# Reordering the opening of a fused HGRN2 encoder layer

## The chip, the cores and the metric

One core of a Trainium2 chip runs the kernel. TensorE (PE) multiplies, VectorE (DVE), ScalarE (ACT) and GpSimd (POOL) do elementwise work, and SyncE (SP) issues the loads and stores. The time is device microseconds of one execution, the median of several runs.

## The reference

Two sequences (1024 and 256 tokens of 1024 channels, f32) pass through one layer with the same weights:

```python
shift, scale, gate = split(silu(c) @ ada_w + ada_b, 3)          # c: one row for each sequence
h = rms(x) * norm_g * (1 + scale) + shift
q, f_fw, f_bw, i, z = split(h @ hg_w_in, 5)                      # 1024 x 10240, 16 heads of 128
lb = cumsum(softmax(hg_lb, 0), 0)[0]
f = lb + (1 - lb) * sigmoid(f_raw); k = 1 - f; g = log(f)        # for each direction
o = gated_chunkwise(silu(q), k_fw, i, g_fw) + flip(gated_chunkwise(flipped ...))
y = (rms(o) * norm_g2 * silu(z)) @ hg_w_out
out = rms(x + gate * y) * final_g
```

## The kernel before

Products in f32 are made as three products of split operands: each of h and w is cast to a high part, and the low part is the difference (`hi*hi + hi*lo + lo*hi`). `split_w` (L113) splits a weight block: a ScalarE copy makes the high part, a POOL subtraction the low part. `make_h` (L184) modulates two of the eight 128-channel blocks of one segment of tokens and splits them: one block is modulated on ScalarE (L191), cast on VectorE (L193) and its low part made on POOL (L195); the other goes VectorE (L192), ScalarE (L194), VectorE (L196). The tokens form three segments of 512, 512 and 256 (si = 0, 1, 2).

The opening (L228 to L325) is written under a manual schedule: each engine takes its instructions in the order of the text, SP its loads too. It does this:

- Small rows are loaded (`crow`: the conditioning; `lbrow`: the forget-gate bounds; `abn`: bias and norm gain), then x in blocks j of 128 tokens (`load_x`, tile `xj`, 4 buffers) and raw weight blocks (`fetch_raw`, tile `raw`, 2 buffers).
- `norm_x(j)` (L161): ScalarE squares a block and takes the root of its mean (L167, L168), VectorE takes the reciprocal and scales the block in place (L169, L170).
- `transpose_x(j)` (L172): eight TensorE transpositions in two halves, each into a PSUM bank; VectorE copies the first half to `xT`, ScalarE the second (L181).
- `load_mod(r)`, `mod_mm(r)`, `mod_tr(r)`: shift and scale of channel blocks 2r and 2r+1 (r = 0 to 3). Four loads of 512 KB (tile `aw`, 7 buffers), 64 small TensorE products, a VectorE copy, a TensorE transposition and two small VectorE instructions that write `mod`.
- `first_project(r, accs)` (L219): for each pair (i, si), six products (two channel blocks, three part products) of weight block i (0 is `wq`, 1 is `wff`) with segment si. All r add up in six banks `p_acc` (`pf` in the trace).

In the order before, `row(j)` normalises block j+2, transposes block j and loads block j+4; all eight blocks of the long sequence go first, with the loads of `aw0`, `wff` and part of `aw1` among them. Then come `mod_mm(0)`, `make_h` for r = 0, the first products, blocks 8 and 9, and three rounds, each with `mod_mm(r)`, `make_h` of the three segments and 36 products. The third weight block, `wv`, is split in two parts, the first in round 3, the second (into the weight buffer of `wq`, there being three) in the middle of the last products. The softmax of the forget-gate bounds (L309 to L325) ends the opening.

After it the main part begins with the product `pv` (L443). There TensorE's order is again that of the text, and a planner orders the other engines. PSUM has eight banks: three with tag pj, two tu, two sc, one ob. A tile waits for a buffer of its tag to come free.

Of the kernel before, what the change touches and what calls it, by code (L numbers as in the profile page):

```python
# [9 lines left out]
F32 = mybir.dt.float32  # L10
# [7 lines left out]
DRAM = bass.MemoryType.DRAM  # L18

P = 128  # L20
# [17 lines left out]
LEAD = 5  # L38
# first and last 128-token blocks of the two sequences
FIRST = (0, 8)  # L40
# [4 lines left out]
def kernel(  # L45
# [38 lines left out]

# [1 line left out]
    ident = const.tile([P, P], F32, name="ident")  # L86
# [32 lines left out]

    # weight blocks in the order in which the tensor engine takes them  # L120
    order = []
# [22 lines left out]

# [1 line left out]
    p0 = tc.alloc_tile_pool(name="p0", bufs=1)  # L146
# [4 lines left out]
    def load_x(j):  # L151
        xts[j] = p0.tile([P, D], F32, tag="xj", bufs=4, name=f"xj{j}")
        sp.dma_start(xts[j], xs[j])

    def load_mod(r, pieces=range(4)):
        # shift and scale of two of the eight channel blocks
        for k0, i in [(0, 0), (0, 1), (4, 0), (4, 1)][pieces[0]:pieces[-1] + 1]:
            aws[r, k0, i] = p0.tile([P, 4, 256], F32, tag="aw", bufs=7, name=f"aw{r}_{k0}_{i}")
            sp.dma_start(aws[r, k0, i], ada3[:, k0:k0 + 4, i * D + r * 256:i * D + (r + 1) * 256])

    def norm_x(j):  # L161
        """128 rows of x over their rms."""
        xj = xts[j]
        sq = p0.tile([P, D], F32, tag="sq", bufs=1, name=f"sq{j}")
        ssum = p0.tile([P, 1], F32, tag="ssum", bufs=4, name=f"ssum{j}")
        rst = p0.tile([P, 1], F32, tag="rst", bufs=4, name=f"rst{j}")
        act.activation(sq, xj, AF.Square, accum_out=ssum)  # L167
        act.activation(rst, ssum, AF.Sqrt, bias=eps_t, scale=1.0 / D)  # L168
        dve.reciprocal(rst, rst)  # L169
        dve.tensor_scalar_mul(xj, xj, rst)  # L170

    def transpose_x(j):  # L172
        xj = xts[j]
        si = min(j // 4, 2)
        c = slice(j * P - SEGS[si][0], (j + 1) * P - SEGS[si][0])
        for h in range(2):
            xp = ps.tile([P, 512], F32, tag=("tu", "sc")[h], bufs=2, name=f"xp{j}_{h}")
            for i in range(4):
                k = 4 * h + i
                pe.transpose(xp[:, i * P:(i + 1) * P], xj[:, k * P:(k + 1) * P], ident)  # L180
            (act.copy if h else dve.tensor_copy)(  # L181
                xT[si][:, 4 * h:4 * h + 4, c], xp.rearrange("p (i c) -> p i c", i=4))

    def make_h(si, r):  # L184
        """Channel blocks 2 r and 2 r + 1 of the modulated rows, split in two parts."""
        grp = 0 if SEGS[si][0] < TP else 1
# [11 lines left out]
    def mod_mm(r):  # L198
        # two channel blocks of shift and scale in four column tiles
        acc = mod_ps[:, (r % 2) * 256:(r % 2) * 256 + P]  # L200
# [8 lines left out]
    def mod_tr(r):  # L209
        tr = mod_ps[:, (r % 2) * 256 + P:(r % 2 + 1) * 256]  # L210
        pe.transpose(tr, mrows[r], ident)
        # mod[:, s, i, r]: shift of channel block i, then norm_g * (1 + scale), for prompt and sample
        i2 = slice(2 * r, 2 * r + 2)
# [5 lines left out]
    def first_project(r, accs):  # L219
        """Part of the projections by the first two weight blocks."""  # L220
        for i, si in accs:
# [6 lines left out]
    with tc.manual_schedule():  # L228
        crow = p0.tile([2 * KT, P], F32, name="crow")
        sp.dma_start(crow[:KT], c_prompt.rearrange("o (k p) -> (o k) p", p=P))  # L230
        sp.dma_start(crow[KT:], c_sample.rearrange("o (k p) -> (o k) p", p=P))
        lbrow = p0.tile([2 * NH + 1, P], F32, name="lbrow")
        sp.dma_start(lbrow[:2 * NH], hg_lb.rearrange("l (h p) -> (l h) p", p=P))
        sp.dma_start(lbrow[2 * NH:], hg_norm_g)
        abn = p0.tile([24, P], F32, name="abn")
        sp.dma_start(abn[:16], ada_b[0, :2 * D].rearrange("(a p) -> a p", p=P))
        sp.dma_start(abn[16:], norm_g.rearrange("o (a p) -> (o a) p", p=P))
        for j in range(4):
            load_x(j)
        raws[0] = fetch_raw(0)  # L240

        lb_ps = tu_bank("lb_ps")
        pe.transpose(lb_ps[:, 96:112], crow, ident[:16, :16])
        act.activation(csT, lb_ps[:, 96:112].rearrange("p (c k) -> p k c", c=2), AF.Silu)
        pe.transpose(lb_ps[:, :2 * NH + 1], lbrow, ident[:2 * NH + 1, :2 * NH + 1])
        pe.transpose(lb_ps[:, 64:88], abn, ident[:24, :24])
        dve.tensor_copy(lbT, lb_ps[:, :2 * NH + 1])
        abT = p0.tile([P, 3, KT, 1], F32, name="abT")
# [3 lines left out]

        def row(j):
            if j + 2 < 8:
                norm_x(j + 2)
            transpose_x(j)
            if j + 4 < NT:
                load_x(j + 4)

        norm_x(0)  # L260
        norm_x(1)
        for j in range(8):
            row(j)
            if j == 2:
                split(0, raws[0])
            if j == 3:
                load_mod(0)
                raws[1] = fetch_raw(1)
            if j == 5:
                load_mod(1, (0, 1, 2))  # L270
            if j == 6:
                split(1, raws[1])
        mod_mm(0)
        load_mod(1, (3,))
        mod_tr(0)
        make_h(0, 0)
        make_h(1, 0)
        for i in range(2):
            p_acc[i, 0] = pj_bank(f"pf{i}_0")
        norm_x(8)  # L280
        norm_x(9)
        first_project(0, ((0, 0), (1, 0)))
        row(8)
        row(9)
        for i in range(2):
            p_acc[i, 1] = ps.tile([P, 512], F32, tag="sc", bufs=2, name=f"pf{i}_1")
        make_h(2, 0)
        for i in range(2):
            p_acc[i, 2] = tu_bank(f"pf{i}_2")[:, :256]
        for r in range(1, 4):  # L290
            mod_mm(r)
            if r < 3:
                load_mod(r + 1)
            first_project(r - 1, ((0, 1),))
            mod_tr(r)
            if r == 3:
                raws[2] = fetch_raw(2)
                wv = [split_w(*raws[2][0])]
            for si in range(3):
                make_h(si, r)  # L300
            first_project(r - 1, ((1, 1), (0, 2), (1, 2)))
            if r < 3:
                first_project(r, ((0, 0), (1, 0)))
        first_project(3, ((0, 0), (0, 1), (0, 2), (1, 0)))
        ready[2] = wv + [split_w(*raws[2][1])]
        first_project(3, ((1, 1), (1, 2)))

        # forget-gate lower bound: softmax over the two rows of hg_lb
        e0 = p0.tile([P, NH], F32, name="e0")  # L309
# [9 lines left out]
        dve.tensor_tensor(e0, e0, e1, ALU.mult)  # L319
        # sigmoid(x) = (1 + tanh(x / 2)) / 2; the factor 2 of silu is kept in q and taken out of k  # L320
        dve.tensor_scalar(f_scale, e0, -0.5, 0.5, ALU.mult, ALU.add)
# [5 lines left out]
    def gate_rows():  # L327
        """The gate of the residual branch, kept in DRAM until the last phase."""
        aws, acc = {}, []
# [30 lines left out]

# [1 line left out]
    pp = tc.alloc_tile_pool(name="pp", bufs=1, reuse_waits="tile")  # L362
# [91 lines left out]
    def gates(e, d):  # L454
        """Decays of one direction and the key factors."""
        for si in seg_order["ff" if d == 0 else "fb"]:
# [4 lines left out]
        for si in seg_order["ff" if d == 0 else "fb"]:  # L461
# [21 lines left out]
            dec_t[e, d, si] = ds_  # L483
            # of two neighbouring chunks, the later queries in scan order meet the earlier keys
            # directly, and both meet the state at the start of the pair
            dve.tensor_tensor(x4[:, :, ca], u4[:, :, ca], k4[:, :, ca], ALU.mult)
# [18 lines left out]
    def attention(e):  # L505
        """Pieces of one head's attention, in the order in which the tensor engine takes them."""
        kts, sc_bank = {}, {}
# [65 lines left out]
        def out(b):  # L573
# [3 lines left out]
            if si not in obs:  # L577
                if si == 2:
                    # the free half of the bank of the scores
                    obs[si] = sc_bank[0][:, 2:].rearrange("p n c -> p (n c)")  # L580
                else:
                    obs[si] = ps.tile([P, 512], F32, tag="ob", bufs=1, name=f"ob{e}_{si}")
                left[si] = sl // P
# [49 lines left out]

# [1 line left out]
    HALF = NH // 2  # L635
# [47 lines left out]
    with tc.manual_schedule(engines={PE}):  # L683
# [5 lines left out]
        gates(0, 0)  # L689
        # two banks of scores: what no product writes is masked and only has to hold something  # L690
        sc_banks = [ps.tile([P, 4, P], F32, tag="sc", bufs=2, name=f"sc{i}") for i in range(2)]
# [138 lines left out]
```

## Time and profile before

| | us |
|---|---|
| median of 3 runs | 1742.09 (1742.04 to 1742.49) |
| span of the profiled execution | 1741.6 |
| PE busy | 1692.4 (97%) |
| DVE busy | 1014.0 (58%) |
| ACT busy | 775.8 (45%) |
| POOL busy | 578.6 (33%) |

The profiled execution's own time is not listed apart from its span, from the first to the last instruction; the median of the runs lies 0.5 us above it. Busy shares are averages over a span in which the opening and the main part differ. Rows of the timeline give the start in us, the duration, the engine, the line, and in brackets the idle time before with what ended it. Matmuls overlap, so the distance of two starts is the cost of one in a row of them.

### The profile page before, as it was taken

The numbers are of one execution on the slowest core, as the hardware profiler recorded it, in microseconds if no ns is written. First come the engines' busy times: TensorE is split into PE (matmuls) and PEld (weight loads), VectorE is DVE, ScalarE is ACT, GpSimd is POOL, SyncE is SP. The second block draws the span as 40 slices with busy tenths as digits, with TensorE's granted clock in tenths as the row PEclk, the third lists the DMA queues.
The fourth block names the chain that finished last, engine by engine and source line by source line (L and its number), as shares of the span: only waits on it lengthen the run. The fifth ranks groups of instructions, "written<-read, shape, count | busy, mean of one in ns | idle before, by whom it ended". The sixth has DMA issues, their size and how long they took to land.

```text
span 1741.6 us, 28354 instructions
## 1 busy us (share of the span) xinstructions
PE 1692.4 (97%) x11511; PEld 1461.6 (84%) x11511; DVE 1014.0 (58%) x2223; ACT 775.8 (45%) x1197; POOL 578.6 (33%) x547
## 2 busy tenths in 40 slices
PE   5999999999999999999999999999999999899998
PEld 4797789888988898889888998889888988788886
DVE  5646664667566754764477447744775466834322
ACT  5443534463545454545454435533463446542210
POOL 1532433352334233433344334333333333610000
PEclk8999999999999999999999999999999999999999
DMA  8311311011011011111111111111111100564310
GB/s 279 121 38 62 98 34 43 28 41 36 25 52 37 28 37 40 37 40 37 40 31 46 31 43 34 34 37 38 36 40 34 43 17 13 169 209 153 123 51 27
DMA packets 121268, 103.06 MB, mean 59 GB/s; under 512 B 3929, under 2 KB 108466, under 8 KB 121138
## 3 DMA queue, kind: packets, MB, share of 16 engines
q1 hardware_dynamic: 121138, 101.26, 18.3%
q8 instruction: 90, 1.47, 0.3%
q14 instruction: 40, 0.33, 0.1%
HBM read 85.50 MB, written 15.74 MB: 58 GB/s over the span
## 4 chain that ended last, share of the span: by engine, by line
PE 70%; DVE 19%; ACT 3%; issue 3%; DMA 0%; POOL 0%; DVEq 0%; ACTq 0%; POOLq 0%
PE pv L443 13%; PE pfb L421 12%; PE y L674 12%; PE pff L421 12%; PE pq L421 7%; PE pz L421 3%; PE ob L592 3%; DVE g L466 3%; DVE ku L473 2%; DVE qe L472 2%; PE sc L550 2%; DVE ke L489 2%; PE up L531 1%; DVE s L538 1%; PE kt L519 1%
## 5 line engine op out<-in xcount | busy, mean ns | idle before, releaser
L443 PE MATMUL pv<-wv_h,h_hi 128*128 128x256 f32 x640 | 181.2, 283 | 0.0
L443 PE MATMUL pv<-wv_l,h_hi 128*128 128x256 f32 x640 | 181.1, 283 | 0.0
L443 PE MATMUL pv<-wv_h,h_lo 128*128 128x256 f32 x640 | 181.1, 283 | 0.0
L522 DVE COPY kts<-kt 128x512 f32<-128x512 f32 (+2 forms) x96 | 48.3, 503 | 204.3 <-PE kt L519 204.3
L487 POOL TENSOR_TENSOR ku<-xx,dec 128x256 f32<-128x256 f32 (+1 forms) x96 | 74.7, 779 | 230.1 <-DVE dec L480 151.6
L466 DVE TENSOR_TENSOR_SCAN g<-reset,g 128x512 f32<-128x512 uint8 (+1 forms) x96 | 100.8, 1075 | 83.8 <-ACT g L458 83.8
L421 PE MATMUL pz<-h_hi,wz_h 128*128 128x512 f32 (+1 forms) x384 | 148.5, 387 | 0.0
L421 PE MATMUL pff<-h_hi,wff_h 128*128 128x512 f32 (+1 forms) x360 | 141.6, 393 | 0.0
L421 PE MATMUL pq<-h_hi,wq_h 128*128 128x512 f32 (+1 forms) x360 | 141.1, 392 | 0.0
L421 PE MATMUL pz<-h_hi,wz_l 128*128 128x512 f32 (+1 forms) x384 | 136.7, 356 | 0.0
L421 PE MATMUL pz<-h_lo,wz_h 128*128 128x512 f32 (+1 forms) x384 | 136.5, 356 | 0.0
L421 PE MATMUL pfb<-h_hi,wfb_h 128*128 128x512 f32 (+1 forms) x384 | 136.2, 355 | 0.0
L421 PE MATMUL pfb<-h_lo,wfb_h 128*128 128x512 f32 (+1 forms) x384 | 136.0, 354 | 0.0
L421 PE MATMUL pfb<-h_hi,wfb_l 128*128 128x512 f32 (+1 forms) x384 | 135.8, 354 | 0.0
L421 PE MATMUL pq<-h_hi,wq_l 128*128 128x512 f32 (+1 forms) x360 | 128.6, 357 | 0.0
L421 PE MATMUL pff<-h_hi,wff_l 128*128 128x512 f32 (+1 forms) x360 | 128.6, 357 | 0.0
L421 PE MATMUL pq<-h_lo,wq_h 128*128 128x512 f32 (+1 forms) x360 | 128.2, 356 | 0.0
L421 PE MATMUL pff<-h_lo,wff_h 128*128 128x512 f32 (+1 forms) x360 | 128.1, 356 | 0.0
L615 POOL TENSOR_TENSOR z<-z,rs 128x512 f32<-128x512 f32 (+1 forms) x48 | 54.1, 1127 | 212.2 <-ACT rs L614 211.0
L443 PEld LDWEIGHTS pv<-wv_l,h_hi 128*128 128x128 f32 x640 | 122.9, 192 | 0.0
L443 PEld LDWEIGHTS pv<-wv_h,h_lo 128*128 128x128 f32 x640 | 122.9, 192 | 0.0
L443 PEld LDWEIGHTS pv<-wv_h,h_hi 128*128 128x128 f32 x640 | 122.9, 192 | 0.0
(196 smaller groups left out, 4598.9 us busy)
## 6 DMA issues: line engine op xcount, KB each, us to landing
xj<-in_x_prompt_dram SPq DMA_DIRECT2D x16, 512.0 KB, 4.5
wq_r<-in_hg_w_in_dram SPq DMA_DIRECT2D x16, 512.0 KB, 3.8
aw<-in_ada_w_dram SPq DMA_DIRECT2D x16, 512.0 KB, 10.2
wff_r<-in_hg_w_in_dram SPq DMA_DIRECT2D x16, 512.0 KB
wv_r<-in_hg_w_in_dram SPq DMA_DIRECT2D x16, 512.0 KB, 3.5
wfb_r<-in_hg_w_in_dram SPq DMA_DIRECT2D x16, 512.0 KB
wz_r<-in_hg_w_in_dram SPq DMA_DIRECT2D x16, 512.0 KB
wo_r<-in_hg_w_out_dram SPq DMA_DIRECT2D x16, 512.0 KB, 4.7
```

Source lines behind the costliest of these rows:

```text
L421: pe.matmul(acc[:, :sl], a[:, k, :], h[si][:, k, :], start=n == 0, stop=n == 3 * KT - 1)
L443: pe.matmul(acc[:, :2 * P], h[si][:, k, c], a[:, k % 4, :], start=n == 0, stop=n == 3 * KT - 1)
L466: dve.tensor_tensor_scan(gs, reset[:, :sl], gs, 0.0, ALU.mult, ALU.add)
L472: dve.tensor_tensor(chunks(qe), g3, g3[:, :, mid:mid + 1].broadcast_to([P, nch, C]), ALU.subtract)
L473: dve.tensor_tensor(chunks(ku), g3[:, :, last:last + 1].broadcast_to([P, nch, C]), g3, ALU.subtract)
L487: pool.tensor_tensor(u4[:, :, ca], x4[:, :, ca], dec[:, :, cb].broadcast_to([P, nb, C]), ALU.mult)
L489: (pool if e == NH - 1 and d == 1 else dve).tensor_tensor(ke, ke, k, ALU.mult)
L522: dve.tensor_copy(kt[:, c], tp[:, c])
L550: pe.matmul(sps[c * C:(c + 1) * C, i, c * C:(c + 1) * C], ke[:, o:o + C], qe[:, o:o + C], start=True, stop=True)
L592: pe.matmul(ob[:, c], l, r, start=n == 0, stop=n == len(ops) - 1)
L615: pool.tensor_tensor(u, u, rs, ALU.mult)
L674: pe.matmul(y_bank(j, n), u[:, e % HALF, :], w[e][:, n * 512:(n + 1) * 512], start=first and e == 0, stop=last and e == NH - 1)
```

## The change

The loads of `abn` and of the first modulation weights (`load_mod(0)`) are issued ahead of x, six blocks of x can be loaded at once instead of four and eight pieces `aw` instead of seven, and `lbrow` is loaded later. The reserve in on-chip memory for descriptors written by software falls to 1024 bytes a partition. `mod_mm(0)` is issued ahead of the first block of x; the transpositions use the banks tu and pj instead of tu and sc, since the banks sc now belong to `p_acc[i, 1]` from the beginning. The loop of rows gives way to a list in which normalisation, transposition, modulation, `make_h` and first products alternate. In addition, comments and docstrings are removed.

```diff
-        xts[j] = p0.tile([P, D], F32, tag="xj", bufs=4, name=f"xj{j}")
+        xts[j] = p0.tile([P, D], F32, tag="xj", bufs=6, name=f"xj{j}")
...
-            aws[r, k0, i] = p0.tile([P, 4, 256], F32, tag="aw", bufs=7, name=f"aw{r}_{k0}_{i}")
+            aws[r, k0, i] = p0.tile([P, 4, 256], F32, tag="aw", bufs=8, name=f"aw{r}_{k0}_{i}")
...
-            xp = ps.tile([P, 512], F32, tag=("tu", "sc")[h], bufs=2, name=f"xp{j}_{h}")
+            xp = tu_bank(f"xp{j}_{h}") if (2 * j + h) % 3 else pj_bank(f"xp{j}_{h}")
...
+        load_mod(0)
+        for j in range(4):
+            load_x(j)
+        raws[0] = fetch_raw(0)
+        for j in range(4, 6):
+            load_x(j)
+        load_mod(1)
         lbrow = p0.tile([2 * NH + 1, P], F32, name="lbrow")
...
-        def row(j):
-            if j + 2 < 8:
-                norm_x(j + 2)
-            transpose_x(j)
-            if j + 4 < NT:
-                load_x(j + 4)
-
+        mod_mm(0)
         norm_x(0)
         norm_x(1)
-        for j in range(8):
-            row(j)
-            if j == 2:
-                split(0, raws[0])
-            if j == 3:
-                load_mod(0)
-                raws[1] = fetch_raw(1)
-            if j == 5:
-                load_mod(1, (0, 1, 2))
-            if j == 6:
-                split(1, raws[1])
-        mod_mm(0)
-        load_mod(1, (3,))
+        transpose_x(0)
+        load_x(6)
         mod_tr(0)
+        norm_x(2)
+        transpose_x(1)
+        load_x(7)
+        norm_x(3)
+        transpose_x(2)
+        raws[1] = fetch_raw(1)
+        load_x(8)
+        split(0, raws[0])
+        norm_x(4)
+        transpose_x(3)
+        load_x(9)
+        load_mod(2)
         make_h(0, 0)
+        norm_x(5)
+        transpose_x(4)
+        first_project(0, ((0, 0),))
+        transpose_x(5)
+        mod_mm(1)
+        load_mod(3)
+        norm_x(6)
+        mod_tr(1)
+        transpose_x(6)
+        norm_x(7)
+        make_h(0, 1)
+        transpose_x(7)
+        split(1, raws[1])
         make_h(1, 0)
-        for i in range(2):
-            p_acc[i, 0] = pj_bank(f"pf{i}_0")
+        first_project(1, ((0, 0),))
+        first_project(0, ((1, 0), (0, 1)))
         norm_x(8)
         norm_x(9)
-        first_project(0, ((0, 0), (1, 0)))
-        row(8)
-        row(9)
-        for i in range(2):
-            p_acc[i, 1] = ps.tile([P, 512], F32, tag="sc", bufs=2, name=f"pf{i}_1")
+        make_h(1, 1)
+        first_project(1, ((1, 0),))
+        transpose_x(8)
+        transpose_x(9)
+        first_project(0, ((1, 1),))
         make_h(2, 0)
+        raws[2] = fetch_raw(2)
+        pe.transpose(lb_ps2 := mod_ps[:, 128:128 + 2 * NH + 1], lbrow, ident[:2 * NH + 1, :2 * NH + 1])
+        dve.tensor_copy(lbT, lb_ps2)
+        mod_mm(2)
+        first_project(1, ((0, 1),))
+        mod_tr(2)
...
-        for r in range(1, 4):
-            mod_mm(r)
-            if r < 3:
-                load_mod(r + 1)
-            first_project(r - 1, ((0, 1),))
-            mod_tr(r)
-            if r == 3:
-                raws[2] = fetch_raw(2)
-                wv = [split_w(*raws[2][0])]
-            for si in range(3):
-                make_h(si, r)
-            first_project(r - 1, ((1, 1), (0, 2), (1, 2)))
-            if r < 3:
-                first_project(r, ((0, 0), (1, 0)))
-        first_project(3, ((0, 0), (0, 1), (0, 2), (1, 0)))
+        make_h(0, 2)
+        make_h(2, 1)
+        first_project(1, ((1, 1),))
+        make_h(1, 2)
+        first_project(0, ((0, 2), (1, 2)))
+        wv = [split_w(*raws[2][0])]
+        first_project(2, ((0, 0), (1, 0)))
+        mod_mm(3)
+        make_h(2, 2)
+        first_project(1, ((0, 2), (1, 2)))
+        mod_tr(3)
+        first_project(2, ((0, 1),))
+        for si in range(3):
+            make_h(si, 3)
+        first_project(2, ((1, 1), (0, 2), (1, 2)))
+        first_project(3, ((0, 0), (1, 0)))
         ready[2] = wv + [split_w(*raws[2][1])]
-        first_project(3, ((1, 1), (1, 2)))
+        first_project(3, ((0, 1), (1, 1), (0, 2), (1, 2)))
...
-    nc = _bacc.Bacc("TRN2", target_bir_lowering=False, num_devices=1)
+    nc = _bacc.Bacc("TRN2", target_bir_lowering=False, num_devices=1, dynamic_dma_scratch_size=1024)
```

## Rows read from the trace of the kernel before

**Rows 1.** Busy time by stretch: opening and rest (us; engines, granted clock, DMA share, GB/s).
```profile
0.00:80.00 80.00, 57.88 (x493) 46.73 (x494) 47.12 (x88) 41.92 (x75) 26.22 (x25) 0.89 0.63 205
80.00:1741.60 1661.60, 1634.53 (x11021) 1414.82 (x11019) 966.92 (x2136) 733.87 (x1123) 552.35 (x524) 1.00 0.17 52
```
**Rows 2.** Busy time by stretch: two of 5 us in the opening.
```profile
20.00:25.00 5.00, 3.54 (x17) 2.96 (x16) 3.90 (x8) 4.35 (x10) 1.27 (x1) 0.50 1.01 352
...
35.00:40.00 5.00, 4.07 (x9) 2.89 (x10) 4.50 (x6) 3.12 (x7) 2.78 (x2) 0.50 1.10 349
```
**Rows 3.** Waits, 0 to 90 us: who waited for whom, us, times, longest.
```profile
PE xp L180 <- DVE xj L170: 6.0, 1, 6.0
...
ACT sq L167 <- DMA xj<-in_x_prompt_dram: 5.0, 4, 3.3
ACT wff_h L116 <- DMA wff_r<-in_hg_w_in_dram: 4.4, 1, 4.4
```
**Rows 4.** Timeline: the first block of x, from its load to its copy.
```profile
2.97 1.78 SPq L153 DMA_DIRECT2D xj<-in_x_prompt_dram  x4
...
6.51 1.06 ACT L167 ACTIVATE sq<-xj 128x1024 f32<-128x1024 f32 x1 [3.33 <-DMA xj<-in_x_prompt_dram]
...
7.74 1.28 ACT L168 ACT_TABLE_LOAD   x1
...
10.37 5.26 PE L180 MATMUL xp<-ident,xj 128*128 128x128 f32 x24 [5.97 <-DVE xj L170]
...
12.37 0.59 ACT L181 COPY xT<-xp 128x512 f32<-128x512 f32 x1 [0.31 <-PE xp L180]
```
**Rows 5.** Timeline of PE: two later groups of eight transpositions.
```profile
15.98 1.10 PE L180 MATMUL xp<-ident,xj 128*128 128x128 f32 x8 [0.35 <-DVE xT L181]
...
19.06 1.97 PE L180 MATMUL xp<-ident,xj 128*128 128x128 f32 x8 [1.98 <-DVE xT L181]
```
**Rows 6.** Timeline: a weight split on POOL beside a scaling on DVE.
```profile
18.92 2.36 POOL L117 TENSOR_TENSOR wq_l<-wq_r,wq_h 128x1024 fp32r<-128x1024 f32 x1 [17.55 <-ACT wq_h L116]
...
20.44 1.38 DVE L170 TENSOR_SCALAR xj<-xj,rst 128x1024 f32<-128x1024 f32 x1
```
**Rows 7.** Timeline: low part of make_h(1,0) on POOL; first products at two pitches.
```profile
37.19 1.29 POOL L195 TENSOR_TENSOR h_lo<-xT,h_hi 128x512 fp32r<-128x512 f32 x1 [0.70 <-DVE h_hi L193]
...
37.56 0.63 PE L225 MATMUL pf<-h_hi,wq_h 128*128 128x512 f32 x1
...
37.99 0.63 PE L225 MATMUL pf<-h_lo,wq_h 128*128 128x512 f32 x1
...
53.16 0.39 PE L225 MATMUL pf<-h_hi,wff_h 128*128 128x512 f32 x1
53.39 0.40 PE L225 MATMUL pf<-h_lo,wff_h 128*128 128x512 f32 x1
```
**Rows 8.** Timeline: third modulation product, its addition, a low part behind it, first pv.
```profile
53.95 1.93 PE L203 MATMUL mod_ps<-aw,csT 128*2 128x128 f32 x64
...
57.62 0.17 DVE L215 TENSOR_TENSOR mod<-mod_ps,abT 128x8 f32<-128x8 f32 x1 [1.38 <-PE mod_ps L211]
...
64.39 0.74 POOL L195 TENSOR_TENSOR h_lo<-xT,h_hi 128x256 fp32r<-128x256 f32 x1 [1.16 <-DVE h_hi L193]
...
79.39 0.28 PE L443 MATMUL pv<-wv_h,h_hi 128*128 128x256 f32 x1
```
**Rows 9.** Timeline: second part of wv, softmax, q's evacuation.
```profile
76.05 1.05 ACT L116 CAST wv_h<-wv_r 128x1024 fp32r<-128x1024 f32 x1 [1.46 <-PE pf L225]
...
77.18 2.40 POOL L117 TENSOR_TENSOR wv_l<-wv_r,wv_h 128x1024 fp32r<-128x1024 f32 x1 [2.01 <-ACT wv_h L116]
...
78.77 0.84 DVE L317 TENSOR_TENSOR e<-e,e 128x16 f32<-128x16 f32 x1 [2.93 <-ACT e L316]
...
81.09 0.69 DVE L405 SCALAR_TENSOR_TENSOR q<-q,pf 128x512 f32<-128x512 f32 x1
```
**Rows 10.** Waits of PE, 80 us to the end: the largest.
```profile
PE kt L519 <- DVE s L538: 6.9, 16, 1.0
```

More of the change, by code (lines that the diff above doesn't have):

```diff
@@ L231 @@
         sp.dma_start(crow[KT:], c_sample.rearrange("o (k p) -> (o k) p", p=P))
+        abn = p0.tile([24, P], F32, name="abn")
+        sp.dma_start(abn[:16], ada_b[0, :2 * D].rearrange("(a p) -> a p", p=P))
+        sp.dma_start(abn[16:], norm_g.rearrange("o (a p) -> (o a) p", p=P))
+        load_mod(0)
[5 more added lines that the diff above has]
+        load_mod(1)
         lbrow = p0.tile([2 * NH + 1, P], F32, name="lbrow")
@@ L234 @@
         sp.dma_start(lbrow[2 * NH:], hg_norm_g)
[L235 to L240, printed above, removed]
         lb_ps = tu_bank("lb_ps")
@@ L244 @@
         act.activation(csT, lb_ps[:, 96:112].rearrange("p (c k) -> p k c", c=2), AF.Silu)
-        pe.transpose(lb_ps[:, :2 * NH + 1], lbrow, ident[:2 * NH + 1, :2 * NH + 1])
         pe.transpose(lb_ps[:, 64:88], abn, ident[:24, :24])
-        dve.tensor_copy(lbT, lb_ps[:, :2 * NH + 1])
         abT = p0.tile([P, 3, KT, 1], F32, name="abT")
@@ L251 @@
         dve.memset(mod_ps, 0.0)
-        def row(j):
-            if j + 2 < 8:
-                norm_x(j + 2)
-            transpose_x(j)
-            if j + 4 < NT:
-                load_x(j + 4)
+        for i in range(2):
+            p_acc[i, 0] = pj_bank(f"pf{i}_0")
+            p_acc[i, 1] = ps.tile([P, 512], F32, tag="sc", bufs=2, name=f"pf{i}_1")
+        mod_mm(0)
         norm_x(0)
         norm_x(1)
-        for j in range(8):
-            row(j)
-            if j == 2:
-                split(0, raws[0])
-            if j == 3:
-                load_mod(0)
-                raws[1] = fetch_raw(1)
-            if j == 5:
-                load_mod(1, (0, 1, 2))
-            if j == 6:
-                split(1, raws[1])
```

## The prediction

> **What bounds the kernel now.** I read the busy time by stretch first. After 80 us TensorE is busy 1634.5 of 1661.6 us; before that, 57.9 of 80 [rows 1]. The order after 80 us is not edited, so the question is when the first product of the third weight block (`pv`) can start: 79.39 us now [rows 8]. Next the waits of the opening: ScalarE waits 5.0 us for rows of x and 4.4 us for the raw `wff`, and TensorE 6.0 us before its first transposition [rows 3]. The stretches show loads at 349 to 352 GB/s with the engines' share at or over 1 [rows 2], so 512 KB take 1.5 us. Thus the first half of the opening waits for loads. The change attacks these; what counts is which wait ends last in their place.
>
> **Loads.** The 16 `aw` pieces, ten x blocks and four raw weight loads are the same 15.7 MB. Four `aw` loads now precede x: 4 x 1.5 = 6.0 us, less 0.7 us for the two `lbrow` issues moved behind. x0 landed at 6.51, when its Square started [rows 4]; it will land near 11.8. `aw0` lands near 10.2, and the first modulation product (1.93 us at full clock [rows 8]) ends before x0 is normalised. At 1.5 us a load x4 lands at 19, `aw1` at 27, x7 at 30, `wff` at 31, `aw3` at 46 to 48. SP's later issues wait for transpositions of rows 0 to 3 and for the second modulation product, which come before their place in that stream or at most some 2 us after it. So no wait for loads remains behind x0. The reduced descriptor reserve only makes room for the buffers; every load is issued on SP's queue. I cost it at nothing: the queue's waits, not POOL, would show if that were wrong.
>
> **Chain to the first half of h.** Every engine takes its list in order, so I follow it.
> - x0 to first transposition took 3.86 us including one table load of 1.28 [rows 4]; so transposition at 15.7, and 2.5 us per later row from Square to transposition. Eight transpositions take 1.10 us at full clock and 1.97 at half [rows 5]; a ScalarE copy 0.59, Square 1.06 [rows 4].
> - Before, rows were normalised two ahead. Now ScalarE holds the order copy 0, norm 2, copy 1, norm 3, copy 2, cast of wq, norm 4. The copy of row 0 starts at 17.6, Square 2 at 18.1, its transposition at 20.6; copy 2 at 21.7 to 22.5 (by the clock), the cast of wq, Square 4 at 23.2 to 24.0.
> - `wq_l` then runs on POOL, 2.36 us. The row scale that began under such a piece took 1.38 us and ended 0.54 us after it [rows 6]; so scale 4 ends at 26.2, and copy 3 (VectorE) behind it at 26.8. make_h(0,0) needs this copy; its low part ends near 30.1.
> - The first product group holds TensorE behind that low part: six products at 0.43 us pitch (half clock [rows 7]), to 32.4. Transposition 5 is queued behind it (34.1), copy 5 and with it Square 6 behind that (34.9). Before, these rows met no product.
> - mod_mm(1) is next, 34.1 to 36.8 (1.9 at full clock, nearly twice that at half by the ratio in [rows 5]; I take 2.7). Its copy stands ahead of scale 6 on VectorE: scale 6 at 38.1, transposition 6 at 39.0, Square 7 at 39.8, scale 7 at 42.2.
> - make_h(0,1) ends on VectorE at 45.0, copy 7 at 45.5. The cast of wff lets `wff_l` occupy POOL from 45.0 to 47.3, so both VectorE pieces of make_h(1,0) end at 47.6 and 48.0. Its low part (1.29 us [rows 7]) ends at **49.3**.
>
> The same piece ended at 37.19 + 1.29 = 38.5 before [rows 7]: 10.8 us later. In exchange TensorE has by then done the second modulation product and two groups that came later before. Transpositions now share three PSUM banks instead of four; each half waits for the copy three halves earlier, which at this pace has ended, so up to row 7 this costs nothing.
>
> **From there to the product pv.** TensorE's work left at 49.3 is the rest of one group (1.2) and 28.6 us: 12 wide groups of six products at 0.23 (16.6; the pitch at full clock [rows 7]), 8 narrow ones at half that (5.7), two modulation products (3.8), 16 transpositions at 0.11 (1.8) and 0.7 of small ones. Dense, it would end at 79.1. But VectorE and POOL also have rows 8 and 9 to scale, make_h(1,1) and make_h(2,0). Row 9's second half waits for a TU bank: 0.5 us if it takes the bank that ScalarE frees, 2.1 if the one that VectorE frees; I take 0.5, since a bank freed earlier is nearer to what the row order of the copies gives. The scale for channel blocks 4 and 5 is added at 59.4 against 57.62 [rows 8]. From that instruction to pv it took 79.39 - 57.62 = 21.8 us. The new order has one half-size make_h more there (1.6 us: 0.74 on POOL [rows 8] and three pieces on VectorE), and the third modulation addition no longer waits for TensorE (1.4 us); I take 21.7, and 20 to 23.5 as ends. pv can start at **81.1**, 1.7 later.
>
> **The end of the opening.** `wv` part 1 takes wq's weight buffer. Before, all wq products were issued ahead of four last wff groups, and the cast at 76.05 left `wv_l` ready at 79.58 [rows 9]. pv needs it 13 products of 0.12 after its start, 80.95: 1.4 us to spare. Now wq's (0,2) is next to last: it ends 0.7 before pv may start, and `wv_l` takes another 3.5 us from cast to end. It arrives at 81.1 - 0.6 + 3.5 = 84.0, needed at 82.7: a new stall of **1.4 us**. The softmax follows that cast on ScalarE, so q's evacuation (VectorE row at 81.09 [rows 9]) falls 2.6 us further behind and pv's second bank comes 0.1 to 0.8 late: **0.4**. These two edits are ordered wait for wait; the bounds are 0 and 2.4.
>
> **Sum.** +1.7 + 1.4 + 0.4 = +3.5 us on a profiled span of 1741.6, hence 1745.1. The median of the runs, 1742.09, lies 0.5 above the span; so 1745.6. `lbT`'s move (two small instructions, under mod_mm) and the comments cost nothing. The planner that orders the other engines after the opening may settle differently: TensorE's largest wait there is 6.9 us in 16 pieces [rows 10]; I take 0, with 2 either way.
>
> The clock has a rule against it. Rows of TensorE: eight transpositions at 15.98 ran at full clock after a dense run of 24, those at 19.06 at half after an idle stretch [rows 5]. The Trainium skill, "TensorE: Matmul & The Clock Gate", Part 4: PE-mode transpose, says that the full clock does not engage for transposes. This trace disagrees: the dense run brought it on. By that rule all eight rows would run at half clock, pv would be some 0.7 us later and the sum 1746.3.
>
> **Rivals.**
> 1. *Not slower: the VectorE/POOL holds don't fall on the chain.* If `wq_l` and `wff_l` slip into gaps of VectorE, 1.3 + 0.5 + 2.1 us go; with full clock from row 2 on another 2.7 go. Then make_h(1,0) is ready at 49.3 - 6.6 = 42.7; TensorE, dense, starts pv at 72.5; with the 1.8 at the end that is 5.1 less: 1737.0. It decides if that low part ends before 45. For it: loads no longer stop ScalarE [rows 3]. Against: each weight split sits beside a VectorE piece in the new list, and the row of [rows 6] shows the hold. Loads alone would allow still less (`aw3` at 46 + 15.4 us of tail as now, 61).
> 2. *Slower yet: half clock to 40 us and the bank that comes late.* 0.7 + 0.9 for mod_mm(1) at half clock + 1.6 for row 9: 1748.8. For it: by the steps above TensorE is idle about half of 12 to 30 us, and idle stretches brought the half clock back [rows 2, 5]. Against: products and modulation come denser from 32 us.
> 3. *No change: full clock with the holds.* 2.7 less: 1742.9. The moved work would merely exchange a wait on loads for one on the row chain.
>
> **How the numbers follow.** The forecast (own range 1742 to 1748.5) 0.50, rival 1 0.25, rival 2 0.15, rival 3 0.10. 0.2% is 3.5 us, about what a measurement here tells from no change. The forecast lies on that edge: 0.27 of its 0.50 are over it, 0.23 under. Slower 0.27 + 0.15 = 0.42, same 0.23 + 0.10 = 0.33, faster 0.25. The range, 1735 to 1751, holds rival 1 at its computed value with 2 us for the planner, and rival 2 with the same.
>
> **What would show it.** x0's Square near 11.8, no ScalarE wait for `wff_r`; row scale 4 over 1.3 us; transposition 5 behind the first product group; make_h(1,0)'s POOL piece ending near 49; pv at 80 to 82, with a wait on POOL `wv_l` some 13 products in. I am wrong if that POOL piece ends before 45, or if pv starts before 76.

## The result, and the profile after

The changed kernel takes **1753.6 us** (median of 4 runs, 1753.0 to 1754.6); before, measured beside it, takes 1742.3. The ratio is 1.0063 [1.0049, 1.0078]: 11.3 us slower, where 3.5 were forecast. The execution in the profile took 1753.0 us with a span of 1751.3. Each run of both kernels whose span is listed lies about 1.7 us above it. The profile of before, with a span of 1741.6, was therefore itself an execution of some 1743.3 us, 1.2 above its median.

From the first `pv` to the end, TensorE's 11024 products come in the same order in both kernels, so their starts can be compared one by one. The offset is +4.4 us at the first `pv` (83.79 against 79.39), +5.8 behind its 13th product, +8.3 behind its 24th and +9.7 at its 38th; then it stays between 9.7 and 10, but for some 200 products between 8.5 and 10.2, and ends at 9.7. All that is lost at the end was lost before 94 us.

Busy time by stretch (answers to [rows 1] and, with the two stretches of 5 us, to [rows 2]):
```profile
0.00:80.00 80.00, 54.97 (x465) 42.02 (x466) 44.92 (x81) 38.47 (x70) 23.11 (x21) 0.94 0.62 205
80.00:1751.30 1671.30, 1639.33 (x11048) 1418.97 (x11046) 969.89 (x2143) 737.29 (x1128) 554.85 (x526) 1.00 0.17 52
...
20.00:25.00 5.00, 3.80 (x16) 3.07 (x16) 3.03 (x6) 3.78 (x8) 0.22 (x1) 1.00 1.10 349
35.00:40.00 5.00, 4.03 (x77) 2.79 (x75) 2.36 (x7) 1.93 (x4) 0.00 (x0) 0.92 1.09 343
```
The opening moves the same 205 GB/s as before, and the engines do less in it: TensorE 2.9 us, ScalarE 3.5, POOL 3.1. Between 20 and 25 us the loads run as fast as before (349 against 352 GB/s), but VectorE and ScalarE are busy 3.0 and 3.8 us instead of 3.9 and 4.4. The loads that come first are now those of the modulation weights, and x0 comes at 12.2 us instead of 6.5.

Waits from 0 to 95 us (who waited for whom: us, times, longest), beside [rows 3], which ends at 90:
```profile
PE xp L180 <- DVE xj L170: 10.9, 5, 3.3
ACT sq L167 <- DMA xj<-in_x_prompt_dram: 9.1, 1, 9.1
PE pv L464 <- DVE vt L470: 2.3, 1, 2.3
PE pv L464 <- POOL wv_l L117: 1.2, 1, 1.2
```
ScalarE's several waits for x have become one of 9.1 us, its wait for `wff` is gone, TensorE waits for a scaled row five times instead of once, and two waits stand inside `pv` that the kernel before did not have.

The row chain, timeline (start, duration, engine, line, operation, in brackets the idle time before and what ended it), answering [rows 4 to 7]:
```profile
12.23 1.06 ACT L167 ACTIVATE sq<-xj 128x1024 f32<-128x1024 f32 x1 [9.06 <-DMA xj<-in_x_prompt_dram]
...
24.78 2.34 POOL L117 TENSOR_TENSOR wq_l<-wq_r,wq_h 128x1024 fp32r<-128x1024 f32 x1 [23.41 <-ACT wq_h L116]
...
26.30 1.37 DVE L170 TENSOR_SCALAR xj<-xj,rst 128x1024 f32<-128x1024 f32 x1
...
27.73 1.09 PE L180 MATMUL xp<-ident,xj 128*128 128x128 f32 x8 [2.74 <-DVE xj L170]
...
33.42 0.63 PE L225 MATMUL pf<-h_hi,wq_l 128*128 128x512 f32 x1
33.85 1.91 PE L180 MATMUL xp<-ident,xj 128*128 128x128 f32 x8
...
35.80 0.58 ACT L181 COPY xT<-xp 128x512 f32<-128x512 f32 x1 [4.32 <-PE xp L180]
36.28 1.06 ACT L167 ACTIVATE sq<-xj 128x1024 f32<-128x1024 f32 x1
...
40.06 0.58 ACT L181 COPY xT<-xp 128x512 f32<-128x512 f32 x1 [2.30 <-PE xp L180]
40.54 1.06 ACT L167 ACTIVATE sq<-xj 128x1024 f32<-128x1024 f32 x1
...
46.73 2.38 POOL L117 TENSOR_TENSOR wff_l<-wff_r,wff_h 128x1024 fp32r<-128x1024 f32 x1 [1.57 <-ACT wff_h L116]
...
47.40 2.00 DVE L193 CAST h_hi<-xT 128x512 fp32r<-128x512 f32 x1 [0.51 <-ACT xT L191]
...
49.48 1.68 POOL L195 TENSOR_TENSOR h_lo<-xT,h_hi 128x512 fp32r<-128x512 f32 x1 [0.36 <-DVE h_hi L193]
```
Read it as a chain: x0 is there at 12.2; the scale of row 4 lies behind `wq_l` (1.37 us); row 5's transposition stands behind the six products on TensorE; ScalarE copies row 5 at 35.80 and only then, next in its list, squares row 6 (36.28), and likewise row 7 (40.54). `wff_l` holds VectorE's cast, and the low part of `make_h(1,0)` ends at 51.16.

The end of the opening (same columns), answering [rows 8, 9]; after it no wait of TensorE is longer in sum than the 6.7 us for `s`, 6.9 before [rows 10]:
```profile
61.94 0.17 DVE L215 TENSOR_TENSOR mod<-mod_ps,abT 128x8 f32<-128x8 f32 x1 [1.38 <-PE mod_ps L211]
...
83.20 1.05 ACT L116 CAST wv_h<-wv_r 128x1024 fp32r<-128x1024 f32 x1 [2.92 <-PE pf L225]
...
83.79 0.28 PE L464 MATMUL pv<-wv_h,h_hi 128*128 128x256 f32 x1
...
84.32 2.36 POOL L117 TENSOR_TENSOR wv_l<-wv_r,wv_h 128x1024 fp32r<-128x1024 f32 x1 [3.46 <-ACT wv_h L116]
...
86.74 0.38 PE L464 MATMUL pv<-wv_l,h_hi 128*128 128x256 f32 x1 [1.23 <-POOL wv_l L117]
...
86.89 2.37 POOL L117 TENSOR_TENSOR wfb_l<-wfb_r,wfb_h 128x1024 fp32r<-128x1024 f32 x1 [0.21 <-ACT wfb_h L116]
...
87.04 2.26 DVE L340 TENSOR_TENSOR e<-e,e 128x16 f32<-128x16 f32 x1
...
90.10 0.42 DVE L470 COPY vt<-pv 128x256 f32<-128x256 f32 x1
...
90.43 1.61 DVE L426 SCALAR_TENSOR_TENSOR q<-q,pf 128x512 f32<-128x512 f32 x3
...
90.57 0.58 PE L464 MATMUL pv<-wv_h,h_hi 128*128 128x256 f32 x1 [2.26 <-DVE vt L470]
```
Two things are to be seen. The cast of `wv_h` now begins 0.6 us before `pv` instead of 3.3, so `wv_l` comes late. And behind it stands a chain that no single row gives away: an operation of 128x16 elements (L340), 0.18 us in e1 below, takes 2.26 under `wfb_l`; the copy `vt` stands behind it on VectorE, and the 25th product of `pv` starts 0.05 us after that copy ends.

In the kernel before, that product did not wait for `vt`. Timeline of kernel before:
```profile
82.27 0.28 PE L443 MATMUL pv<-wv_h,h_hi 128*128 128x256 f32 x1
...
83.27 0.42 DVE L449 COPY vt<-pv 128x256 f32<-128x256 f32 x1
```
There VectorE evacuates q first (81.09, [rows 9]) and `vt` after it, and the 25th product (82.27) starts while `vt` is still to come. In the changed kernel the planner puts `vt` ahead of q's three evacuations (90.43), and the product starts while the first of these is still running. So the bank that it takes is not the one that q frees; by the wait it is that of `vt`. A part of the wait would be there without the hold: the last product of the first bank starts at 88.03, and the copy takes 0.42.

### The profile page after: what moved, and what is told of

Same layout as the page of the kernel before. It is cut to its first block, busy times and chain, and to the rows that moved or that the text cites. A ratio compares the mean times of both kernels' runs of the same rounds, so it can differ in the third digit from the quotient of the medians.

```text
span 1751.3 us, 28351 instructions
## 1 busy us (share of the span) xinstructions
PE 1694.3 (97%) x11511; PEld 1461.0 (83%) x11511; DVE 1014.8 (58%) x2223; ACT 775.8 (44%) x1197; POOL 578.0 (33%) x547
## 4 chain that ended last, share of the span: by engine, by line
PE 70%; DVE 20%; ACT 4%; issue 3%; DMA 1%; POOL 1%; SPq 0%; DVEq 0%; ACTq 0%; POOLq 0%
PE pv L464 13%; PE pfb L442 12%; PE y L695 12%; PE pff L442 12%; PE pq L442 7%; PE ob L613 3%; DVE g L487 3%; PE pz L442 3%; DVE ku L494 2%; DVE qe L493 2%; DVE ke L510 2%; PE sc L571 2%; DVE s L559 1%; PE up L552 1%; PE kt L540 1%
```

## The experiments

Eleven kernels ran, in three groups, each group on one chip beside the kernel before (1742.06, 1741.78 and 1741.72 us). Ratios are against before. Effects of a few us are read from the traces, where a part can be placed, and from the medians. With four runs the interval is 2.6 us to each side, so what e6, e7 and e9 show against the changed kernel (0.9 to 3.0 us) rests on their traces.

| kernel | us (runs) | ratio to before | first `pv`, us |
|---|---|---|---|
| changed | 1753.60 (4) | 1.0063 [1.0049, 1.0078] | 83.79 |
| e1 tail back | 1748.92 (4) | 1.0039 [1.0024, 1.0054] | 84.56 |
| e2 reserve alone | 1742.12 (10) | 1.0000 [0.9990, 1.0010] | 78.19 |
| e3 tail alone | 1747.52 (6) | 1.0029 [1.0017, 1.0041] | 77.23 |
| e4 x first | 1748.32 (5) | 1.0035 [1.0022, 1.0049] | 78.92 |
| e5 e1 and e4 | 1744.39 (10) | 1.0015 [1.0005, 1.0024] | 81.19 |
| e6 softmax early | 1750.61 (4) | 1.0051 [1.0036, 1.0066] | 82.94 |
| e7 product later | 1752.70 (4) | 1.0063 [1.0048, 1.0078] | 84.56 |
| e8 loads alone | 1738.41 (10) | 0.9981 [0.9971, 0.9990] | 74.39 |
| e9 norm ahead | 1751.15 (4) | 1.0055 [1.0040, 1.0070] | 80.75 |
| e10 e5 and e9 | 1741.12 (10) | 0.9997 [0.9988, 1.0007] | 77.53 |
| e11 e8, modulation inside | 1737.71 (10) | 0.9978 [0.9968, 0.9987] | 75.35 |

**e1: the last groups as before, in the changed kernel.**
```diff
-        first_project(3, ((0, 0), (1, 0)))
+        first_project(3, ((0, 0), (0, 1), (0, 2), (1, 0)))
         ready[2] = wv + [split_w(*raws[2][1])]
-        first_project(3, ((0, 1), (1, 1), (0, 2), (1, 2)))
+        first_project(3, ((1, 1), (1, 2)))
```


> The changed kernel with only the order of the last product groups as before (all groups of wq ahead of the second split of wv). Theory (the end of the opening costs by itself): pv no longer waits for wv_l (1.4 us), the softmax runs before wfb_l takes POOL, so pv's second bank is free in time (2.5 us), and TensorE keeps its full clock (1.4 us). The narrow wq group may wait up to 1 us for the last low part. pv starts at 83.8 to 84.8, total 1753.6 - 4.3 to 5.3 = 1748.3 to 1749.3. Rival (these waits only mirror a late opening and move elsewhere): 1752.5 to 1754.

1748.92 us, 4.7 less than the changed kernel. In its trace `pv` has no wait, the offset to before is +5.2 at the first `pv` and at most 5.7 later, and the same L340 takes 0.18 us, since `wfb_l` starts behind it. Timeline of kernel e1:
```profile
85.14 0.18 DVE L340 TENSOR_TENSOR e<-e,e 128x16 f32<-128x16 f32 x1
...
86.49 2.42 POOL L117 TENSOR_TENSOR wfb_l<-wfb_r,wfb_h 128x1024 fp32r<-128x1024 f32 x1
```
q is evacuated ahead of `vt` again (86.27 against 88.45). The 5.3 us of stalls and half clock that the changed kernel's trace shows are gone, but `pv` starts 0.8 us later. An earlier `pv` is what the new order gains, set against its stalls: from the end of the last low part (L196) to `pv` it takes 2.7 us in the changed kernel, e4, e6, e7 and e9 (2.0 in e3), and 3.9 in each kernel whose last groups stand as before.

**e2: the smaller descriptor reserve alone, in the kernel before.**
```diff
-    nc = _bacc.Bacc("TRN2", target_bir_lowering=False, num_devices=1)
+    nc = _bacc.Bacc("TRN2", target_bir_lowering=False, num_devices=1, dynamic_dma_scratch_size=1024)
```


> The kernel before with only the descriptor reserve set to 1024 bytes. The changed kernel's runs lie 1.7 us above their span, those of before 0.5. Theory A (the reserve costs the difference outside the span): span 1741.6, runs 1.7 us above it, total 1743.3 to 1743.5. Theory B (the reserve costs nothing, as predicted; the difference belongs to the program's order or its execution): 1742.0 to 1742.5. A span that moves by over 1 us would be a third case, the addresses of tiles.

1742.12 us: no cost shows, within 1.7 us. Its profiled opening is 1.2 us shorter than the one of before (first `pv` at 78.19 against 79.39) at an equal median, which shows how much one execution's opening differs from another's.

**e3: the changed kernel's last groups alone, in the kernel before** (e1's edit the other way round).

> The kernel before with only the changed order of the last product groups. If the end of the opening costs by itself: pv starts at 79.0 to 79.4, waits 1.4 us for wv_l after 13 products, its second bank comes 2 to 2.5 us late behind the softmax on VectorE, and some products run at half clock: 1742.3 + 4 to 5.3 = 1746.3 to 1747.6. As predicted for the end alone (1.4 + 0.4): 1744.1. If the waits only mirror a late opening: 1742 to 1742.5.

1747.52 us, 5.5 more than before. Waits of PE from 70 to 95 us, kernel e3:
```profile
PE pv L443 <- DVE vt L449: 2.3, 1, 2.3
PE pv L443 <- POOL wv_l L117: 1.2, 1, 1.2
```
The two waits are the changed kernel's to the tenth, in a kernel whose loads and rows are as before. Behind them the granted clock from 84 to 88 us is 0.50 (1.2 GHz), which adds 2.5 us here. L319, the softmax step that is L340 in the changed kernel, takes 2.27 us here. So the tail edit is a loss by itself, in the old opening as in the new.

**e4: x ahead of the first modulation weights again.** `mod_mm(0)` and `mod_tr(0)` move with them behind row 3.
```diff
-        load_mod(0)
         for j in range(4):
             load_x(j)
         raws[0] = fetch_raw(0)
+        load_mod(0)
...
-        mod_mm(0)
         norm_x(0)
...
-        mod_tr(0)
         norm_x(2)
...
         load_x(9)
+        mod_mm(0)
+        mod_tr(0)
         load_mod(2)
```


> The changed kernel with four x blocks and wq loaded ahead of the first modulation weights again, and the first modulation product behind the fourth transposition. Theory (the late x0 shifts the whole row chain): x0's Square at 6.7 instead of 12.2, low part of make_h(1,0) near 46 instead of 51.2, pv at 78.5 to 80 instead of 83.8; total 1753.6 - 4 to 5.3 = 1748.3 to 1749.6. Rival (later holds between VectorE and POOL and the order of rows set the end whenever x arrives): the shift shrinks to under 1.5 us by make_h(1,0), total 1752 to 1753.6.

1748.32 us, 5.3 less than the changed kernel. Timeline of kernel e4:
```profile
6.00 1.06 ACT L167 ACTIVATE sq<-xj 128x1024 f32<-128x1024 f32 x1 [2.63 <-DMA xj<-in_x_prompt_dram]
...
44.62 1.68 POOL L195 TENSOR_TENSOR h_lo<-xT,h_hi 128x512 fp32r<-128x512 f32 x1 [0.36 <-DVE h_hi L193]
```
x0's Square starts at 6.00 instead of 12.23 us, the low part of `make_h(1,0)` ends at 46.30 instead of 51.16, and `pv` starts 4.9 us earlier, with both stalls still behind it. The modulation product that moved with x was not what held the rows: in the changed kernel it ends at 12.83, 3.3 us before the first transposition.

**e5: e1 and e4 together.**

> The changed kernel with both edits taken back that cost the most alone: the last groups of the row project as before, and x0 to x3 and wq loaded ahead of the first modulation weights, with their products and transposition behind transpose_x(3). Theory: the two costs are separate (alone they gave 4.7 and 5.3 us back), so pv starts at about 79.7 us and nothing stalls behind it: 1743.6 us (1743 to 1744.5), that is 1.5 over before, which the rest of the change (part (0,0) between the transpositions, wff_r and x loads) costs. Rival: they overlap, since an earlier pv meets the weight casts sooner: 1745 to 1748 us. Rival: the added loads are a gain that the two costs hid: below 1741 us.

1744.39 us; 9.2 of the 11.8 us are back, against 10.0 for the two alone. The costs are nearly separate as medians, and 2.6 us [0.9, 4.2] over before remain.

**e6: the softmax ahead of the last groups.** The block from `e0` to `ng_half` is moved.
```diff
+        e0 = p0.tile([P, NH], F32, name="e0")
+        ...
+        dve.tensor_scalar_mul(ng_half, lbT[:, 2 * NH:2 * NH + 1], 0.5)
         first_project(3, ((0, 0), (1, 0)))
```


> The changed kernel with the softmax block (e0 to ng_half) moved ahead of the first group of first_project(3), right behind make_h(3). Theory: pv's second bank is late because the two-input VectorE step of the softmax (L340, 2.26 us) lies behind GpSimd's low part of wfb, and vt's copy behind it; ahead of the weight casts it finds GpSimd free. The wait for wv_l (1.4 us) stays, the one for the second bank falls from 2.5 to about 0.3 us, and with it part of the half clock behind it: 1749.5 to 1751 us. Rival: the bank is late because ScalarE's evacuations and casts are, or the softmax now holds up the casts of wv: 1752 to 1754 us.

Half of the theory holds. The only wait of PE from 80 to 95 us, kernel e6:
```profile
PE pv L464 <- POOL wv_l L117: 2.7, 1, 2.7
```
The wait for the bank is gone, so the late softmax was its cause. Two things go with it that this run does not separate: nothing of the softmax is held under `wfb_l`, and VectorE evacuates q ahead of `vt` again (82.35 against 89.09), so that the 25th product (88.85) does not take `vt`'s bank. But the other wait grew from 1.2 to 2.7: POOL now takes pieces of the gates (L417) and memory fills ahead of `wv_l`, which starts 1.0 us behind the end of its cast. The half clock stays. From the first `pv` to its 39th product the loss is 4.3 us instead of 5.4, so 1.0 us of the 2.3 came back. The median fell by 3.0, more than this; the rest may lie in openings that differ from one execution to the next.

**e7: the early product later.**
```diff
         transpose_x(4)
-        first_project(0, ((0, 0),))
         transpose_x(5)
...
         transpose_x(6)
+        first_project(0, ((0, 0),))
```


> The changed kernel with part (0,0) of the first products moved from behind transpose_x(4) to behind transpose_x(6). Theory: in its place it holds TensorE's queue at half clock until 33.85 us while row 5's transpositions are ready at about 32, and the rows behind it, and with them the modulation of row block 0's low parts, move by as much: part (1,0)'s low part comes 1.5 to 1.8 us earlier, pv too, 1751.8 to 1752.3 us. Rival: the row chain is set by the loads and by VectorE's normalisation, and TensorE's order is covered: 1753 to 1754 us.

1752.70 us: no gain that can be told from none. In the profiled execution x0 landed 1.8 us later (Square at 14.00), so it is read from the low part of `make_h(0,0)`: from its end to that of `make_h(1,0)` takes 17.5 us instead of 19.7. The product did hold the rows. The gain was given back behind it, timeline of kernel e7:
```profile
46.41 2.38 POOL L117 TENSOR_TENSOR wff_l<-wff_r,wff_h 128x1024 fp32r<-128x1024 f32 x1 [0.71 <-ACT wff_h L116]
...
46.89 2.18 DVE L192 TENSOR_SCALAR xT<-xT,mod 128x512 f32<-128x512 f32 x1
...
49.76 1.58 DVE L196 TENSOR_TENSOR h_lo<-xT,h_hi 128x512 fp32r<-128x512 f32 x1 [0.35 <-ACT h_hi L194]
```
`wff_l` now catches an earlier step of `make_h(1,0)`, and L196 then runs beside the low part on POOL (1.58 us, 0.68 in the changed kernel). `pv` starts 33.8 us behind the low part of `make_h(1,0)` instead of 32.6.

**e8: the deeper loads alone, in the kernel before.** The smaller reserve, six `xj` and eight `aw` buffers, and the loads issued earlier:
```diff
+        for j in range(4, 6):
+            load_x(j)
...
-            if j + 4 < NT:
-                load_x(j + 4)
+            if j < 2:
+                load_x(j + 6)
...
+            if j == 1:
+                raws[1] = fetch_raw(1)
+                load_mod(0)
...
             if j == 3:
-                load_mod(0)
-                raws[1] = fetch_raw(1)
-            if j == 5:
-                load_mod(1, (0, 1, 2))
+                load_x(8)
+                load_x(9)
+                load_mod(1)
...
-        load_mod(1, (3,))
```


> The kernel before with only the deeper loads: a small reserve for the DMA descriptors, six x buffers, eight buffers for modulation weights, x4 and x5 loaded at the start, x6 and x7 behind rows 0 and 1, wff and the first modulation weights behind row 1, x8, x9 and the second ones behind row 3. The order of TensorE's work is that of before. Theory: ScalarE's waits for loads in the opening (5.0 us for x, 4.4 us for wff in before) go, the first products start near 31 us instead of 34.8, pv near 75 instead of 79.4 us, and nothing stalls behind it: 1738 to 1739 us. Rival: the row chain (normalisation on VectorE and ScalarE, transposition at half clock) sets the pace, and the loads were covered: 1741 to 1742.5 us. Rival: the weights arrive sooner but the casts of wv stay where they are and pv's earlier start turns into waits for them: 1740 to 1743 us with stalls in the first 24 products of pv.

1738.41 us, 3.4 less than before [1.7, 5.1]. Kernel e8, the wait of ScalarE for x (0 to 95 us) and the first product:
```profile
ACT sq L167 <- DMA xj<-in_x_prompt_dram: 3.4, 1, 3.4
...
30.95 0.51 PE L225 MATMUL pf<-h_hi,wq_h 128*128 128x512 f32 x1 [1.76 <-DVE h_hi L193]
```
ScalarE's only wait for x is the first (3.4 us), none for `wff`; all eight rows are copied by 27 us and the first product runs at 30.95. The waits for loads in [rows 3] were real, and TensorE did not have to be reordered to remove them.

**e9: rows 6 and 7 normalised earlier, in the changed kernel.**
```diff
         transpose_x(4)
+        norm_x(6)
         first_project(0, ((0, 0),))
         transpose_x(5)
+        norm_x(7)
         mod_mm(1)
         load_mod(3)
-        norm_x(6)
         mod_tr(1)
         transpose_x(6)
-        norm_x(7)
         make_h(0, 1)
```


> The changed kernel with the normalisation of rows 6 and 7 issued earlier: norm_x(6) behind transpose_x(4), norm_x(7) behind transpose_x(5), so that on ScalarE they stand ahead of the copies out of the next transposition (as in before, where they run two rows ahead). Theory: in the changed kernel ScalarE copies row 5 at 35.8 us and only then squares row 6 (36.28), copies row 6 and only then squares row 7 (40.54); ahead of the copies, row 6's transposition comes right behind mod_mm(1) at about 37.6, row 7's at about 39.5 instead of 43.15 us, wff's cast and part (1,0)'s low part 2.5 to 3.8 us earlier: 1750 to 1751 us, with the stalls behind pv unchanged. Rival: rows 6 and 7 are waited for as loads (their x lands late), or pv's start is set behind them by the modulation weights: 1752.5 to 1754 us.

1751.15 us, 2.4 less than the changed kernel. Timeline of kernel e9:
```profile
31.09 0.57 ACT L181 COPY xT<-xp 128x512 f32<-128x512 f32 x1
31.55 1.06 ACT L167 ACTIVATE sq<-xj 128x1024 f32<-128x1024 f32 x1
...
35.50 0.58 ACT L181 COPY xT<-xp 128x512 f32<-128x512 f32 x1 [2.47 <-PE xp L180]
35.98 1.06 ACT L167 ACTIVATE sq<-xj 128x1024 f32<-128x1024 f32 x1
...
42.12 1.05 ACT L116 CAST wff_h<-wff_r 128x1024 fp32r<-128x1024 f32 x1
```
Rows 6 and 7 are squared 4.7 and 4.6 us earlier, `wff` is cast 3.5 earlier, the low part of `make_h(1,0)` ends at 48.19 (-3.0), and `pv` starts 3.0 earlier.

**e10: e5 and e9 together.**

> e5 (last groups and the order of the first loads as before) with the same earlier normalisation of rows 6 and 7. Theory: the three costs add up; e5's transposition of row 7 came at 39.32 us and would come near 35.5, pv near 78: 1740.5 to 1742 us, no difference from before. Rival: with x loaded first, rows 6 and 7 are covered by other work and nothing moves: 1744 us. Rival: the loads are all that is left, 1738.5 us as in e8.

1741.12 us, the same as before. With the three edits taken back the whole loss is gone, though part (0,0) still stands between the transpositions, the modulations are interleaved and the banks are three. It does not reach e8, 2.7 us lower: rows 4 and 6 still wait for x there (1.0 and 2.5 us), since the modulation weights are queued between.

**e11: e8, with the first modulation between rows 6 and 7.**
```diff
             if j == 1:
-                raws[1] = fetch_raw(1)
                 load_mod(0)
+                raws[1] = fetch_raw(1)
...
             if j == 6:
-                split(1, raws[1])
-        mod_mm(0)
+                mod_mm(0)
         mod_tr(0)
         make_h(0, 0)
+        split(1, raws[1])
         make_h(1, 0)
```


> e8 (the kernel before with the deeper loads) with one more step, the interleaving in small: the first modulation weights are loaded ahead of wff, the first modulation's products (mod_mm(0)) stand between the transpositions of rows 6 and 7, and the first modulated row block is made ahead of wff's cast. Theory: in e8 TensorE stood idle from 28.5 to 30.95 us while the modulation row was turned and applied; with its products at about 24 us the first product comes 1.5 to 2.4 us earlier: 1736 to 1737 us. Rival: ScalarE is full until 28 us with the row copies and wff's cast, so the first low part comes no earlier than 30.3 us and the time is e8's: 1738 to 1738.5 us. Rival on the other side: the modulation weights land behind 24 us and hold row 7's transposition on TensorE: over 1739 us.

1737.71 us lies between the theory and the first rival; the trace goes with the rival. The first product runs at 30.96 us against 30.95 in e8. `mod_mm(0)`, at 25.04, ran partly at half clock (2.97 us, 2.06 in e8), row 7's transposition waited for it until 27.94, and so the modulation row is applied at 29.64 as in e8 (29.62). It is not to be told from e8, and both are below before.

## Why the prediction missed

The direction (slower had 0.42 of the chances) and both places were right; three sizes and one reference were not. Measured 1753.6 less predicted 1745.6 is 8.0 us: 2.7 at the start of `pv` (1.9 up to the low part of `make_h(1,0)`, 0.8 behind it), 3.5 in the end of the opening, 1.2 from the profile of before, and 0.6 by which the median of the runs lies above the profiled one. The step that failed is the end of the opening: put at 1.4 + 0.4 with 2.4 as its upper bound, it took 5.3 us, since the bank was waited for 2.5 us and not 0.4, and the clock fell behind the wait.

- **"x0 will land near 11.8"**: 12.2. Right, as was "no wait for loads remains behind x0". What I did not ask is what that place costs: e4 puts it at 5.3 us, more than any other step. In the changed kernel, e4 and e9 `pv` starts 32.6 us behind the low part of `make_h(1,0)` (83.79 - 51.16, 78.92 - 46.30, 80.75 - 48.19; forecast 81.1 - 49.3 = 31.8), so there what delays that piece delays `pv` by as much, x0 included (e7, with 33.8, is an exception).
- **"Copy 3 ... low part ends near 30.1 ... to 32.4"**: 31.5 and 33.85. I put the 1.4 us down to the 0.4 of x0 and to the transpositions of rows 0 to 3, all at half pitch; no run separates them. Row 4's (27.73) were the first at the full one.
- **"Scale 4 behind `wq_l`"**: 1.37 us, from the row of 1.38; right. **"Transposition 5 behind the first product group"** and Square 6 and Square 7 behind the copies: right as steps (36.28 and 40.54; I had 34.9 and 39.8). That scale 6 and transposition 6 came when forecast (38.12 and 38.93; I had 38.1 and 39.0) is luck: transposition 5 ended 1.7 us late, and `mod_mm(1)` took 1.93 us instead of 2.7 and the step from its end to scale 6 0.5 instead of 1.3. I wrote this order down and did not see it as a cost that an edit could take away: e9 puts it at 2.4 to 3.0 us.
- **"low part ends at 49.3"**: 51.16. `wff_l` ended at 49.11, not 47.3, and VectorE's cast with it. The cast of `wff` (45.61) stands on ScalarE behind the copy of row 7, whose transposition (43.15) ran at half pitch.
- **"59.4 + 21.7 = 81.1"**: the second modulation interval fits (21.85 us from 61.94 to 83.79), its beginning was 2.5 late. Row 9's second half waited 0.24 us for its bank, near the 0.5 taken.
- **"A new stall of 1.4 us"** for `wv_l`: 1.38 by the offset. Right. (Behind wq's last products before stand three groups of wff, not four; nothing hangs on it.)
- **"pv's second bank comes 0.1 to 0.8 late: 0.4"**: 2.5. This is the step that failed outright. I took the bank to be the one that q's evacuation frees, as in the kernel before, and the planner's order to stay as it was (0 us, "with 2 either way"); the planner put `vt` ahead of q, and `pv` waited for `vt`. I looked at the softmax only as something ahead of q; `vt` stands behind it on VectorE, and the softmax lies under `wfb_l` on POOL. The row for it was at hand: e at 78.77 took 0.84 us for 128x16 elements beside `wv_l` [rows 9]. e1 and e6, each in its own way, remove this wait, and in both q is evacuated first.
- **The half clock behind the stalls**: left out, 1.4 us (2.5 in e3). I gave the clock a rival for the rows and none for the tail.
- **"The median lies 0.5 above the span"**: every run since lies 1.7 above its own. I had set a median beside the span of another execution.

Of the rivals, the second ("half clock to 40 us and the bank that comes late", 1748.8) came nearest in number and named a late bank and the half clock, but not where they cost: `mod_mm(1)` ran at full pitch (1.93 us at 35.69), of rows 4 to 7 two ran at half pitch (5 and 7) and two at full (4 and 6), row 9's bank came 0.24 late, and the late bank was `pv`'s. The first failed on its own point: the low part ended at 51, not before 45. Its gain from loads existed, 3.4 us in e8; in the changed kernel the place of x in the queue and the order of the work outweighed it.

On the rule about transpositions, the 33 TensorE instructions from 16.09 to 24.99 us run at a pitch of 0.213 us within their groups, and the eight from 27.73 at 0.109. The Trainium skill, "TensorE: Matmul & The Clock Gate", Part 4: PE-mode transpose, says that the full clock does not engage for transposes; this trace again disagrees, but here the first full pitch came later than in before (15.98), behind a pause of 2.7 us between rows.

What stays open: why e10 is 2.7 us over e8 beyond the load waits named, how much of the wait for the bank is the hold under `wfb_l` and how much the planner's order, and whether the two stalls could be removed with the new last groups kept, say by a fourth weight buffer; that was not tried.

## What to carry to other kernels

Put first in a queue what the longest chain waits for: 2 MB of early weights ahead of x cost 5.3 us, although every later load then came in time. When an order is written out by hand, read each engine's list for what stands directly behind a wait; a Square behind a copy cost 2.4 us, and a 128x16 operation under a weight split was part of a wait of 2.3. After an edit look also at what a planner reordered behind it: here it changed which copy the next bank came from. Change loads and order apart: the loads alone gained 3.4 us, and the changed kernel lies 15 above that (1753.6 - 1738.4), 5.3 of it by the place of x in the queue.

## What was not expected of the hardware

- An operation of 128x16 elements on VectorE with two tensor inputs takes 0.18 us (e1), and 2.26 when POOL's subtraction of 128x1024 starts 0.15 us before it (2.27 in e3); it ends with that subtraction (89.30 and 89.26). So an operation far smaller than the subtraction was held to its end.
- TensorE's first rows of x ran at half pitch in the three kernels read for it (0.213 us a transposition, from 10.4 us in before, 10.5 in e8 and 16.1 in the changed kernel) while the record of the granted clock reads 1.00 for those stretches. Behind a later pause of the changed kernel both agree on half (products 0.43 us apart at 0.50 between 29 and 33 us). In these traces the pitch has to be read at the beginning, not the record.
- Behind the stall of 2.3 us within `pv` the products stood 0.21 us apart instead of 0.12 for 3 us (90.57 to 93.7), although TensorE had been dense before the two stalls; the granted clock reads 0.50 for this stretch, and in e3, behind the same stall, from 84 to 88 us.
- The opening differs by 1.2 us between executions of two kernels whose medians agree (e2 and before). With the same loads and rows, x0's Square starts at 12.23 us in the changed kernel and at 14.00 in e7.
